# Gated linear attention on one core: chunks of 128 tokens with gates summed from the middle, one carried state instead of three

## The chip, the cores and the metric

The kernel runs on one core of one Trainium2 chip. The metric is device time in microseconds (us) of one execution. The kernel before took 1087.53 us, the median of three runs (1085.79 to 1088.14).

## The reference, cut to what matters

The program computes three transformer layers on 256 tokens of width 1024, in f32: a first block (convolution, sparse attention, feed-forward), a layer whose mixer is gated linear attention, and a layer with block attention. The change lies in the mixer of the second one. It has four heads, a key width of 128 and a value width of 256, and a gate per token and key channel:

```python
def gla_mixer(x, w_in, w_gk, b_gk, norm_g, w_out):
    q, k, v, g, gk_low = split_cols(x @ w_in, GLA_COLS)
    log_a = jax.nn.log_sigmoid((gk_low @ w_gk + b_gk).astype(jnp.float32)) / GLA_GATE_NORMALIZER
    q = to_heads(q, GLA_HEADS) * (GLA_DK ** -0.5)
    o = chunk_gla(q, to_heads(k, GLA_HEADS), to_heads(v, GLA_HEADS), to_heads(log_a, GLA_HEADS))
    o = from_heads(rms_norm_2(o.astype(x.dtype), norm_g)) * jax.nn.silu(g)
    return o @ w_out
```

`chunk_gla` evaluates the recurrence S_t = diag(exp(log_g_t)) S_{t-1} + k_t v_t^T, o_t = S_t^T q_t. The reference does so in chunks of 64 tokens: inside a chunk it forms causal scores from q * exp(cum) and k * exp(-cum), where cum is the running sum of the gates from the start of the chunk; between chunks it carries a state that is decayed by the chunk's whole gate and added to by the keys times exp(last - cum). The chunk length is a choice of the algorithm: any length gives the same outputs but for rounding.

## The kernel before, in words

All weights come from HBM as f32 in pieces of 128 x 2048 (`emit_raw`, line 111, three buffers) and each half of a piece, 128 x 1024, is split into a high and a low part: ScalarE writes the high part (`whi`, line 127), VectorE the rest (`wlo`, line 129). A projection is then three fp32r matmuls for every product (lines 168 to 170 where the weights are stationary, lines 174 to 176 where the activations are). The splits run up to five halves ahead of use. Work inside the attention itself uses plain f32 matmuls; each of them shows in the trace as two passes.

PSUM has four tiles for accumulation (`ps_acc`) and four work tiles (`ps_wk`), of 128 x 512 f32 each.

The 256 tokens are two token tiles of 128 (t = 0, 1). In the stage of the linear attention (lines 890 to 1048) the program goes through these steps:

- The q projection (line 938), the low-rank gate input (`pk`, line 943), and for each tile the gate logits (line 950) with their log-sigmoid: three ScalarE operations (lines 953 to 955) and one on VectorE (line 956) give `la`.
- For each tile, on TensorE: the running sum inside the two 64-token chunks of the tile (`pc`, line 960, with the constant matrix `tri`), the sum from a token to the end of its chunk (`pf`, line 961, with `suf`), and the total of each chunk for each head (`pdec`, line 964, four matmuls with two columns). ScalarE takes exponentials of them (line 967: `ecum`, `einv`, `esuf`; line 969: `dec`). ScalarE's order in this part is the program's own (`manual_schedule`); the others are ordered by the compiler's scheduler, by priority in program order.
- The v projection (two halves of 512 columns, line 981) and the k projection, whose evacuation multiplies by `einv` (line 977) and `esuf` (line 978, into `kend`).
- Transposes of the scaled q and k (line 988), copied to SBUF by ScalarE (line 990).
- The state after chunks 0, 1 and 2 (lines 993 to 1005): for each chunk and head one matmul of 64 rows, `kend` with v (line 998); for chunk 0 ScalarE copies the result (line 1002), for the others VectorE multiplies the state before by the decay and adds the new part (line 1004).
- Scores for each tile and head (line 1013), masked by a predicated copy on VectorE (line 1014) into a tile that was set to zero (line 1009). The mask keeps a pair of tokens only if both are in the same 64-token chunk.
- The outputs (lines 1018 to 1038, high priority): for each pair of heads and tile, scores times v (line 1027), plus for each 64-token chunk after the first the read of the state (line 1030), a matmul with 64 stationary columns that adds to 64 of the 128 output rows; then a sum of squares on ScalarE (line 1033), a power on GpSimd (line 226), and a scaling on VectorE (line 1037).
- The gate projection (`evac_g`, line 1043), two halves of 512 columns. Its matmuls depend on nothing of the attention, so the scheduler puts them between the attention's matmuls on TensorE. Its result is multiplied by the outputs and transposed for the output projection (line 1045, `to_T`, lines 238 to 244).

The output projection, a layer norm, the feed-forward part and the third layer follow. The output projection's early weight splits take over SBUF of the stage, among it the tags S0 and S1 of the state tiles.

Of the kernel before, what the change touches and what calls it, by code (L numbers as in the profile page):

```python
# [9 lines left out]
F32 = mybir.dt.float32  # L10
# [38 lines left out]
for _n, _w in (("ident", P), ("mask", 2 * P), ("tri", P), ("suf", P), ("ind", 2), ("m2", META),  # L49
               ("invf", 16), ("cq", L), ("sq", L), ("ci", L), ("si", L)):  # L50
    CST[_n] = _o
    _o += _w
# [25 lines left out]
def tile_hybrid(ctx: ExitStack, tc: tile.TileContext, x, meta, wts, misc, vec, cst, rows, gkw, ng, pos,  # L78
# [124 lines left out]
    tri = cs[:, CST["tri"]:CST["tri"] + P]  # L203
# [702 lines left out]
    V.tensor_scalar(mask_i, tri, 16.0, None, op0=OP.mult)  # L906
# [38 lines left out]
    dec = gp.tile([P, 4, 4], F32, name="dec")  # L945
    pdec = ps_wk()
    with tc.manual_schedule(engines={ENG.Activation}):
# [10 lines left out]
        for t in range(2):  # L958
            pc, pf = ps_wk(), ps_wk()
            PE.matmul(pc, tri, la[t], start=True, stop=True)  # L960
            PE.matmul(pf, suf, la[t], start=True, stop=True)
            for h in range(4):
                c = (h * 2 + t) * 2
                PE.matmul(pdec[:, c:c + 2], la[t][:, h * P:(h + 1) * P], ind, start=True, stop=True)
            for lst, src, s, nm in ((ecum, pc, 1.0, "ec"), (einv, pc, -1.0, "ei"), (esuf, pf, 1.0, "es")):
# [3 lines left out]
        A.activation(dec.rearrange("p a b -> p (a b)"), pdec[:, :16], AF.Exp)  # L969
        A.activation(cssn, cssn, AF.Sin)  # L970
        A.preload_act_table_set("silu_and_others")
    kend = [gp.tile([P, 512], F32, name=f"ke{t}", tag=f"la{t}") for t in range(2)]
# [3 lines left out]
    def evac_k(t, ps):  # L976
        V.tensor_mul(k_tok[t], ps, einv[t])
        V.tensor_mul(kend[t], ps, esuf[t])
# [13 lines left out]
    sts = {}  # L992
    for c in range(3):
        t, o = c // 2, 64 * (c % 2)
        s4 = gp.tile([P, 4, 256], F32, name=f"S{c}", tag=f"S{c}")
        for h in range(4):
            pu = ps_wk()
            PE.matmul(pu[:, :256], kend[t][o:o + 64, h * P:(h + 1) * P], v_tok[t][o:o + 64, h * 256:(h + 1) * 256],
                      start=True, stop=True)
            s = s4[:, h, :]  # L1000
            if c == 0:
                A.activation(s, pu[:, :256], AF.Copy)
            else:
                V.scalar_tensor_tensor(s, sts[c - 1, h], dec[:, h, c:c + 1], pu[:, :256], op0=OP.mult, op1=OP.add)
            sts[c, h] = s
# [13 lines left out]
    for g in range(2):  # L1019
        for t in range(2):  # L1020
            with tc.high_priority():
                po2 = ps_wk()
                st = sc.tile([P, 2, 2], F32, name="st4", tag="st4", bufs=2)
                for a in range(2):
                    h = 2 * g + a
                    po = po2[:, a * 256:(a + 1) * 256]
                    PE.matmul(po, sm[t * 4 + h], v_tok[t][:, h * 256:(h + 1) * 256], start=True, stop=True)
# [251 lines left out]
```

## Time and profile before

| | before |
|---|---|
| median of 3 runs | 1087.53 us (1085.79 to 1088.14) |
| profiled execution, its own time | 1089.07 us |
| span of the profiled execution | 1087.3 us |
| TensorE busy | 1069.2 us, 98% |
| VectorE busy | 741.3 us, 68% |
| ScalarE busy | 602.1 us, 55% |
| GpSimd busy | 39.3 us, 4% |
| instructions, matmul records | 17606, 7042 |

The span goes from the first to the last instruction of the program. The profile's page gives busy time for each engine (PE is TensorE, DVE is VectorE, ACT is ScalarE, POOL is GpSimd; PEld is the weight load of TensorE, which overlaps its matmuls) and the chain of work that ended last, followed back through whatever released each step. Views of the trace list the waits, the busy time in chosen stretches and the instructions in order of time. Matmuls are pipelined: the duration that is shown for one overlaps the next, so neither busy time nor duration is the time that a matmul occupies the array.

### The profile page before, as it was taken

What the parts mean: (1) busy time and instruction counts of PE and PEld (TensorE: products, weight loads), DVE (VectorE), ACT (ScalarE), POOL (GpSimd) and SP (SyncE); (2) the same over time, 40 slices, a digit from 0 to 9 for tenths busy, and PEclk for the clock granted to TensorE, in tenths of its full rate; (3) what the DMA queues carried; (4) which work ended last, traced back from release to release, by engine and by line L of the source; (5) the groups of instructions that cost most, each with busy time, mean ns of one, the idle gap of its engine ahead of it and who ended that gap; (6) DMA issues with size and microseconds to landing.
All of it is one profiled execution on the core that took longest, in us unless ns stands there. A gap on an engine that the chain in (4) does not pass through costs nothing.

```text
span 1087.3 us, 17606 instructions
## 1 busy us (share of the span) xinstructions
PE 1069.2 (98%) x7042; PEld 960.1 (88%) x7042; DVE 741.3 (68%) x1297; ACT 602.1 (55%) x1051; POOL 39.3 (4%) x45
## 2 busy tenths in 40 slices
PE   8999999999999999999999999999999999999997
PEld 7998998899899999977777899999888878999995
DVE  5899999994776767674566645547665666555555
ACT  6896698574555555566361544446256925444440
POOL 0121001100000000000000000000000000000000
PEclk8999999999999999999999999999999999999999
DMA  7885556464354555453434655557254436555541
GB/s 287 258 197 157 194 161 180 119 242 159 136 202 164 193 179 195 169 193 125 153 125 150 229 194 191 178 179 267 101 209 156 152 120 233 194 192 178 180 149 39
DMA packets 33333, 192.37 MB, mean 177 GB/s; under 512 B 3889, under 2 KB 7857, under 8 KB 12002
## 3 DMA queue, kind: packets, MB, share of 16 engines
q1 hardware_dynamic: 28002, 185.02, 49.0%
q0 software_dynamic: 5248, 6.23, 3.6%
q8 instruction: 55, 0.90, 0.3%
q14 instruction: 28, 0.23, 0.1%
HBM read 183.96 MB, written 1.05 MB: 170 GB/s over the span
## 4 chain that ended last, share of the span: by engine, by line
PE 88%; DVE 6%; ACT 2%; issue 2%; DMA 1%; POOL 0%; SPq 0%; DVEq 0%; ACTq 0%; POOLq 0%
PE ps_wk L170 11%; PE ps_wk L169 11%; PE ps_wk L168 11%; PE ps_acc L174 10%; PE ps_acc L175 10%; PE ps_acc L176 10%; PE ps_acc L168 4%; PE ps_acc L169 4%; PE ps_acc L170 4%; DVE wlo L129 1%; PE ps_wk L238 1%; DVE yc L350 1%; PE ps_acc L319 1%; ACT whi L127 1%; PE ps_wk L526 1%
## 5 line engine op out<-in xcount | busy, mean ns | idle before, releaser
L129 DVE TENSOR_TENSOR wlo<-wraw,whi 128x1024 fp32r<-128x1024 f32 x320 | 388.3, 1222 | 208.1 <-ACT whi L127 207.6
L127 ACT ACTIVATE whi<-wraw 128x1024 fp32r<-128x1024 f32 x322 | 337.5, 1059 | 304.2 <-PE ps_wk L169 116.2
L169 PE MATMUL ps_wk<-hT_l,whi 128*128 128x256 f32 (+1 forms) x976 | 274.8, 282 | 0.0
L170 PE MATMUL ps_wk<-hT_h,wlo 128*128 128x256 f32 (+1 forms) x976 | 274.6, 281 | 0.0
L168 PE MATMUL ps_wk<-hT_h,whi 128*128 128x256 f32 (+1 forms) x976 | 274.1, 281 | 0.0
L168 PEld LDWEIGHTS ps_wk<-hT_h,whi 128*128 128x128 f32 x976 | 184.4, 189 | 1.1
L169 PEld LDWEIGHTS ps_wk<-hT_l,whi 128*128 128x128 f32 x976 | 184.0, 189 | 1.4
L170 PEld LDWEIGHTS ps_wk<-hT_h,wlo 128*128 128x128 f32 x976 | 184.8, 189 | 0.3
L174 PE MATMUL ps_acc<-whi,rg_h 128*128 128x512 f32 x328 | 131.0, 400 | 0.0
L175 PE MATMUL ps_acc<-wlo,rg_h 128*128 128x512 f32 x328 | 129.6, 395 | 0.0
L176 PE MATMUL ps_acc<-whi,rg_l 128*128 128x512 f32 x328 | 127.1, 395 | 0.0
L168 PE MATMUL ps_acc<-hT_h,whi 128*128 128x258 f32 (+2 forms) x352 | 102.1, 290 | 0.0
L170 PE MATMUL ps_acc<-hT_h,wlo 128*128 128x258 f32 (+2 forms) x352 | 100.4, 285 | 0.0
L169 PE MATMUL ps_acc<-hT_l,whi 128*128 128x258 f32 (+2 forms) x352 | 100.4, 285 | 0.0
L176 PEld LDWEIGHTS ps_acc<-whi,rg_l 128*128 128x128 f32 x328 | 61.6, 188 | 14.8 <-DVE rg_l L195 0.2
L174 PEld LDWEIGHTS ps_acc<-whi,rg_h 128*128 128x128 f32 x328 | 61.6, 188 | 14.0 <-ACT rg_h L193 0.2
L175 PEld LDWEIGHTS ps_acc<-wlo,rg_h 128*128 128x128 f32 x328 | 61.7, 188 | 12.9
L174 PE MATMUL ps_acc<-whi,hT_h 128*128 128x512 f32 (+1 forms) x184 | 72.1, 392 | 0.0
L176 PE MATMUL ps_acc<-whi,hT_l 128*128 128x512 f32 (+1 forms) x184 | 71.6, 389 | 0.0
L175 PE MATMUL ps_acc<-wlo,hT_h 128*128 128x512 f32 (+1 forms) x184 | 71.3, 387 | 0.0
L169 PEld LDWEIGHTS ps_acc<-hT_l,whi 128*128 128x128 f32 x352 | 66.3, 188 | 0.3
L168 PEld LDWEIGHTS ps_acc<-hT_h,whi 128*128 128x128 f32 x352 | 66.2, 188 | 0.3
(939 smaller groups left out, 1570.5 us busy)
## 6 DMA issues: line engine op xcount, KB each, us to landing
wraw<-in_wts_dram SPq DMA_DIRECT2D x166, 1024.0 KB, 4.9
ysum<-zs POOLq DMA_DIRECT2D x10, 258.0 KB, 7.2
x<-in_x_dram SPq DMA_DIRECT2D x4, 512.0 KB, 3.6
lg<-in_rows_dram SPq DMA_DIRECT2D x4, 512.0 KB, 3.6
lb<-in_rows_dram SPq DMA_DIRECT2D x4, 512.0 KB, 4.6
wraw<-in_wts_dram SPq DMA_DIRECT2D x2, 512.0 KB, 7.0
out_dram<-x SPq DMA_DIRECT2D x4, 256.0 KB, 2.0
mraw<-in_misc_dram SPq DMA_DIRECT2D x1, 576.0 KB, 12.6
```

The source lines that it names most:

```text
L127: A.activation(hi, r, AF.Copy)
L129: V.tensor_sub(lo, r, hi.bitcast(F32))
L168: PE.matmul(ps, wh, xh, start=first, stop=False)
L169: PE.matmul(ps, wh, xl, start=False, stop=False)
L170: PE.matmul(ps, wl, xh, start=False, stop=last)
L174: PE.matmul(ps, xh, wh, start=first, stop=False)
L175: PE.matmul(ps, xh, wl, start=False, stop=False)
L176: PE.matmul(ps, xl, wh, start=False, stop=last)
L238: PE.transpose(pt[:, a, :], src[:, k * P:(k + 1) * P], ident)
L319: PE.matmul(ps[:, :L], w[a][:, k * P:(k + 1) * P], hT[b][:, k, :], start=k == 0 and a + b == 0, stop=k == KT - 1 and a == 1)
L350: tap = V.scalar_tensor_tensor(dst[:, b, :], src[:, b, :], wc[b], dst[:, b, :], op0=OP.mult, op1=OP.add)
L526: PE.matmul(po, vt[j][:, gs], pT[j + 1], start=False, stop=j == t)
```

## The change

The chunk is now a whole token tile of 128 tokens. The running sums of the gates are counted from the middle of the tile: the constant `rel` gives, for a token in the second half, the sum from token 64 up to it, and for one in the first half minus the sum from the token after it up to token 63. Both exponentials, exp(sum) for q and exp(-sum) for k, are then of sums over at most 64 tokens, as before. The mask becomes the plain causal one (made from `suf` in one operation). Only one state is carried, that at the end of tile 0, read by tile 1. So `pf`, `esuf` and `kend` are made for tile 0 alone; `pdec` for tile 1 alone, as the total of the first 64 tokens of tile 1, since the state must be brought to the middle of tile 1. The state is one matmul of 128 rows for each head (two heads in one PSUM tile), copied on ScalarE with the decay as a scale for each row. The state's read for tile 1 is one matmul of 128 columns for each head; tile 0 has none. SBUF tiles S1, S2, the second `esuf` and the second `kend` are gone.

```diff
--- before.py
+++ after.py
@@ -46,7 +46,7 @@
 
 CST = {}
 _o = 0
-for _n, _w in (("ident", P), ("mask", 2 * P), ("tri", P), ("suf", P), ("ind", 2), ("m2", META),
+for _n, _w in (("ident", P), ("mask", 2 * P), ("rel", P), ("suf", P), ("ind", 2), ("m2", META),
                ("invf", 16), ("cq", L), ("sq", L), ("ci", L), ("si", L)):
     CST[_n] = _o
     _o += _w
@@ -200,7 +200,7 @@
     cs = per.tile([P, CST["cq"]], F32, name="cs")
     ident = cs[:, CST["ident"]:CST["ident"] + P]
     vmask = cs[:, CST["mask"]:CST["mask"] + 2 * P]
-    tri = cs[:, CST["tri"]:CST["tri"] + P]
+    rel = cs[:, CST["rel"]:CST["rel"] + P]
     suf = cs[:, CST["suf"]:CST["suf"] + P]
     ind = cs[:, CST["ind"]:CST["ind"] + 2]
     m2 = cs[:8, CST["m2"]:CST["m2"] + META]
@@ -903,7 +903,7 @@
     nc.sync.dma_start(gw, gkw)
     ngb = row_bcast(gp, ng, 256, "ngb", 1)
     mask_i = gp.tile([P, P], I32, name="mask_i")
-    V.tensor_scalar(mask_i, tri, 16.0, None, op0=OP.mult)
+    V.tensor_scalar(mask_i, suf, -16.0, 1.0, op0=OP.mult, op1=OP.add)
     posi = bp.tile([P, 2], I32, name="posi")
     nc.sync.dma_start(posi, pos.rearrange("o (t p) -> p (o t)", p=P))
 
@@ -942,7 +942,7 @@
               k == 0, k == KT - 1)
     A.activation(gkT[0:16, :], pk[:16, :SEQ], AF.Copy)
     la, ecum, einv, esuf = [], [], [], []
-    dec = gp.tile([P, 4, 4], F32, name="dec")
+    dec = gp.tile([P, 4, 2], F32, name="dec")
     pdec = ps_wk()
     with tc.manual_schedule(engines={ENG.Activation}):
         for t in range(2):
@@ -956,26 +956,31 @@
             V.scalar_tensor_tensor(l_, pz, 0.0, z, op0=OP.min, op1=OP.subtract)
             la.append(l_)
         for t in range(2):
-            pc, pf = ps_wk(), ps_wk()
-            PE.matmul(pc, tri, la[t], start=True, stop=True)
-            PE.matmul(pf, suf, la[t], start=True, stop=True)
-            for h in range(4):
-                c = (h * 2 + t) * 2
-                PE.matmul(pdec[:, c:c + 2], la[t][:, h * P:(h + 1) * P], ind, start=True, stop=True)
-            for lst, src, s, nm in ((ecum, pc, 1.0, "ec"), (einv, pc, -1.0, "ei"), (esuf, pf, 1.0, "es")):
+            pc = ps_wk()
+            PE.matmul(pc, rel, la[t], start=True, stop=True)
+            out_ = [(ecum, pc, 1.0, "ec"), (einv, pc, -1.0, "ei")]
+            if t == 0:
+                pf = ps_wk()
+                PE.matmul(pf, suf, la[t], start=True, stop=True)
+                out_.append((esuf, pf, 1.0, "es"))
+            else:
+                for h in range(4):
+                    PE.matmul(pdec[:, 2 * h:2 * h + 2], la[t][:, h * P:(h + 1) * P], ind, start=True, stop=True)
+            for lst, src, s, nm in out_:
                 e = gp.tile([P, 512], F32, name=f"{nm}{t}", tag=f"{nm}{t}")
                 A.activation(e, src, AF.Exp, scale=s)
                 lst.append(e)
-        A.activation(dec.rearrange("p a b -> p (a b)"), pdec[:, :16], AF.Exp)
+        A.activation(dec.rearrange("p a b -> p (a b)"), pdec[:, :8], AF.Exp)
         A.activation(cssn, cssn, AF.Sin)
         A.preload_act_table_set("silu_and_others")
-    kend = [gp.tile([P, 512], F32, name=f"ke{t}", tag=f"la{t}") for t in range(2)]
+    kend = gp.tile([P, 512], F32, name="ke", tag="la0")
     for t in range(2):
         V.tensor_mul(q_tok[t], q_tok[t], ecum[t])
 
     def evac_k(t, ps):
         V.tensor_mul(k_tok[t], ps, einv[t])
-        V.tensor_mul(kend[t], ps, esuf[t])
+        if t == 0:
+            V.tensor_mul(kend, ps, esuf[0])
 
     for nn in range(2):
         xs_cols(hT, lambda t, ps, nn=nn: A.activation(v_tok[t][:, nn * 512:(nn + 1) * 512], ps, AF.Copy))
@@ -989,20 +994,14 @@
             o = gp.tile([P, 4, P], F32, name=f"{nm}T{t}", tag=f"{nm}{t}")
             A.activation(o.rearrange("p a b -> p (a b)"), pt, AF.Copy)
             lst.append(o)
-    sts = {}
-    for c in range(3):
-        t, o = c // 2, 64 * (c % 2)
-        s4 = gp.tile([P, 4, 256], F32, name=f"S{c}", tag=f"S{c}")
-        for h in range(4):
-            pu = ps_wk()
-            PE.matmul(pu[:, :256], kend[t][o:o + 64, h * P:(h + 1) * P], v_tok[t][o:o + 64, h * 256:(h + 1) * 256],
-                      start=True, stop=True)
-            s = s4[:, h, :]
-            if c == 0:
-                A.activation(s, pu[:, :256], AF.Copy)
-            else:
-                V.scalar_tensor_tensor(s, sts[c - 1, h], dec[:, h, c:c + 1], pu[:, :256], op0=OP.mult, op1=OP.add)
-            sts[c, h] = s
+    state4 = gp.tile([P, 4, 256], F32, name="S", tag="S0")
+    for h in range(0, 4, 2):
+        pu = ps_wk()
+        for a in range(2):
+            PE.matmul(pu[:, a * 256:(a + 1) * 256], kend[:, (h + a) * P:(h + a + 1) * P],
+                      v_tok[0][:, (h + a) * 256:(h + a + 1) * 256], start=True, stop=True)
+        for a in range(2):
+            A.activation(state4[:, h + a, :], pu[:, a * 256:(a + 1) * 256], AF.Copy, scale=dec[:, h + a, 0:1])
     sm = []
     for t in range(2):
         mt4 = gp.tile([P, 4, P], F32, name=f"sm{t}", tag=f"es{t}")
@@ -1024,11 +1023,9 @@
                 for a in range(2):
                     h = 2 * g + a
                     po = po2[:, a * 256:(a + 1) * 256]
-                    PE.matmul(po, sm[t * 4 + h], v_tok[t][:, h * 256:(h + 1) * 256], start=True, stop=True)
-                    for c in range(2):
-                        if 2 * t + c > 0:
-                            PE.matmul(po[64 * c:64 * c + 64], qd[t][:, h, 64 * c:64 * c + 64],
-                                      sts[2 * t + c - 1, h], start=False, stop=True, skip_group_check=True)
+                    PE.matmul(po, sm[t * 4 + h], v_tok[t][:, h * 256:(h + 1) * 256], start=True, stop=t == 0)
+                    if t == 1:
+                        PE.matmul(po, qd[t][:, h, :], state4[:, h, :], start=False, stop=True)
                     sq = bp.tile([P, 512], F32, name="sqw")
                     A.activation(sq[:, :256], po, AF.Square, accum_out=st[:, a, 0:1])
                 r = rsqrt(st[:, :, 1], st[:, :, 0], 1.0 / 256, EPS)
@@ -1240,10 +1237,10 @@
     i = np.arange(P)
     put("ident", np.eye(P, dtype=f))
     put("mask", np.concatenate([np.zeros((P, P)), np.where(i[None, :] <= i[:, None], 0.0, NEG)], axis=1))
-    same = (i[:, None] // 64) == (i[None, :] // 64)
-    put("tri", ((i[:, None] <= i[None, :]) & same) / 16.0)
-    put("suf", ((i[:, None] > i[None, :]) & same) / 16.0)
-    put("ind", (i[:, None] // 64 == np.arange(2)[None, :]) / 16.0)
+    a, b = i[:, None], i[None, :]
+    put("rel", (((a >= P // 2) & (a <= b)) * 1.0 - ((a < P // 2) & (a > b)) * 1.0) / 16.0)
+    put("suf", (a > b) / 16.0)
+    put("ind", np.repeat(a < P // 2, 2, axis=1) / 16.0)
     put("m2", np.where(np.arange(META)[None, :] <= META - 2 + np.arange(8)[:, None] % 2, 0.0, NEG))
     put("invf", np.tile((f(500000.0) ** (-np.arange(0, 32, 2, dtype=f) / f(32)))[None], (P, 1)))
     p = np.arange(L, dtype=f)
```

## Rows read from the trace of the kernel before

**Rows 1.** The page: busy time of each engine, and the chain that ended last by engine.
```profile
PE 1069.2 (98%) x7042; PEld 960.1 (88%) x7042; DVE 741.3 (68%) x1297; ACT 602.1 (55%) x1051; POOL 39.3 (4%) x45
...
PE 88%; DVE 6%; ACT 2%; issue 2%; DMA 1%; POOL 0%; SPq 0%; DVEq 0%; ACTq 0%; POOLq 0%
```

**Rows 2.** Windows of the stage: stretch, length, busy us (instructions), TensorE's granted clock, DMA share, GB/s.
```profile
486.00:550.00 64.00, 64.00 (x296) 47.01 (x295) 32.96 (x63) 32.77 (x59) 2.80 (x4) 1.00 0.37 132
535.80:541.00 5.20, 5.20 (x28) 3.12 (x26) 0.52 (x3) 0.47 (x2) 0.00 (x0) 1.00 0.00 0
541.00:549.00 8.00, 8.00 (x35) 4.63 (x35) 3.17 (x10) 3.33 (x14) 2.10 (x3) 1.00 0.00 0
```

**Rows 3.** Waits from 486 to 570 us: total, times, longest.
```profile
ACT whi L127 <- PE ps_acc L176: 11.2, 14, 5.4
...
ACT we0h L127 <- DMA wraw<-in_wts_dram: 1.6, 1, 1.6
```

**Rows 4.** TensorE's timeline, 490 to 497 us: start, length, engine, line, operation, tiles.
```profile
492.71 0.95 PE L964 MATMUL ps_wk<-cs,la 128*128 128x2 f32 x8
493.52 1.10 PE L960 MATMUL ps_wk<-la,cs 128*128 128x512 f32 x2
494.46 1.02 PE L961 MATMUL ps_wk<-la,cs 128*128 128x512 f32 x2
495.32 0.95 PE L964 MATMUL ps_wk<-cs,la 128*128 128x2 f32 x8
```

**Rows 5.** TensorE's timeline, 526 to 550 us.
```profile
529.16 4.60 PE L998 MATMUL ps_wk<-v,ke 64*128 64x256 f32 x24
533.69 0.94 PE L1013 MATMUL ps_wk<-ecT,eiT 128*128 128x128 f32 x6
534.38 0.48 PE L176 MATMUL ps_acc<-whi,hT_l 128*128 128x512 f32 x1
534.70 1.28 PE L1013 MATMUL ps_wk<-ecT,eiT 128*128 128x128 f32 x10
...
536.05 1.89 PE L1027 MATMUL ps_wk<-v,sm 128*128 128x256 f32 x8
537.87 1.94 PE L1030 MATMUL ps_wk<-S,ecT 128*64 128x256 f32 x12
539.74 0.70 PE L1027 MATMUL ps_wk<-v,sm 128*128 128x256 f32 x2
540.37 0.65 PE L1030 MATMUL ps_wk<-S,ecT 128*64 128x256 f32 x2
540.94 0.50 PE L175 MATMUL ps_acc<-wlo,hT_h 128*128 128x512 f32 x1
...
542.77 0.65 PE L1030 MATMUL ps_wk<-S,ecT 128*64 128x256 f32 x4
543.36 0.50 PE L174 MATMUL ps_acc<-whi,hT_h 128*128 128x512 f32 x1
```

**Rows 6.** Matmuls of L1027 and L1013: passes, duration ns min/median/max, first and last start.
```profile
L1027 PE MATMUL ps_wk<-v,sm x16: 378/379/483, 536.0 to 547.4; 128*128 128x256 f32 x16
...
L1013 PE MATMUL ps_wk<-ecT,eiT x16: 271/275/377, 533.7 to 535.7; 128*128 128x128 f32 x16
```

**Rows 7.** VectorE's timeline, 520 to 550 us.
```profile
531.24 3.22 DVE L1004 SCALAR_TENSOR_TENSOR S<-S,dec,ps_wk 128x256 f32<-128x256 f32 x8 [0.44 <-PE ps_wk L998]
534.38 1.94 DVE L1014 COPY_PREDICATED sm<-mask_i,ps_wk 128x128 f32<-128x128 int32 x8
```

**Rows 8.** ScalarE's timeline, 526 to 550 us.
```profile
527.00 1.06 ACT L127 ACTIVATE whi<-wraw 128x1024 fp32r<-128x1024 f32 x1 [0.33 <-PE ps_acc L176]
...
528.92 1.09 ACT L990 ACTIVATE eiT<-ps_wk 128x512 f32<-128x512 f32 x2
529.90 1.68 ACT L1002 ACTIVATE S<-ps_wk 128x256 f32<-128x256 f32 x4
```

**Rows 9.** ScalarE's scaled products of L367: count, duration ns min/median/max, shapes.
```profile
L367 ACT ACTIVATE zs<-hp,dwh x48: 482/495/520, 34.3 to 196.6; 128x258 f32<-128x258 f32 x20, 128x256 f32<-128x256 f32 x4, 128x248 f32<-128x248 f32 x4, 128x244 f32<-128x244 f32 x4
```

## The prediction

> **What bounds the kernel now.** I read the page first. TensorE is busy for 1069.2 us, 98% of the span, and the chain that ended last is 88% TensorE [rows 1]. A sum over the whole span says nothing about one stage, so the second view is the windows of the stage that the change edits. From 486 to 550 us TensorE is busy for all 64.0 us, VectorE for 33.0 and ScalarE for 32.8, the clock is granted in full, and the DMA share falls to 0.00 in both of its last stretches [rows 2]. So the weights stand ready there: the loads wait for buffers, not the buffers for loads. The waits say the same from the other side: ScalarE's weight splits wait 11.2 us in total for TensorE to give back a buffer, and only once, for 1.6 us, for a load [rows 3]. Here a microsecond that TensorE no longer needs should be a microsecond of the span, and work taken from VectorE or ScalarE should be worth nothing by itself.
>
> A busy share doesn't say how long a matmul holds the array, because its shown duration includes a tail that overlaps the next one. So I price by the TensorE timeline, from the start of one group to the start of the next [rows 4, 5]. An f32 matmul appears there as two passes; the counts below are passes. Three steps are needed. A full-array pass of 256 columns: the eight L1027 passes take 1.89 us, the last has the usual 0.38 [rows 6], so seven steps are 1.51, or **0.216 us** each. A 128-column score pass: ten take 1.28, the last 0.28 [rows 6], so (1.28 - 0.28) / 9 = 0.11. And the change of array shape: the first step after a change costs about 0.1 more. L1013's first six take 0.94, so five steps are 0.66 and not 0.56; from the last full L1027 pass (536.05 + 7 x 0.216 = 537.56) to the first L1030 pass it is 0.31 and not 0.216; the L1027 pair after L1030 takes 0.70, so its step is 0.32 [rows 5].
>
> **The change part by part, on TensorE.**
> 1. The suffix sum of the second token tile goes. L961 for tile 1 runs from 494.46 to 495.32 [rows 4]: **-0.86**.
> 2. The chunk totals of tile 0 go: L964's eight two-column passes from 492.71 to 493.52 [rows 4]: **-0.81**. Tile 1 keeps its eight. They stood between the cumulative sums of the two tiles, so L960 of tile 1 now comes at about 492.7 and needs the gates of tile 1; if those are late, projection passes stand behind it in the queue. I put nothing on this, and the bound is the 0.81 itself.
> 3. The state updates: 24 passes of 64 rows become 8 of 128 rows. Before, they run from 529.16 to 533.69, 4.53 us; after, 8 x 0.216 = 1.73, so -2.80. Both changes of shape around them go too, L988 to L998 and L998 to L1013, some 0.1 each: **-3.0** [rows 5].
> 4. The reads of the state: 24 passes with 64 output columns become 8 with 128, in the shape of L1027, and tile 0 needs none. The block of twelve takes 537.87 to 539.74 = 1.87 and becomes 4 x 0.216 = 0.86, with two changes of shape: -1.2. A pair for tile 0 (540.37 to 540.94, 0.57) goes with its two changes of shape: -0.77, and there are two of these. A four for tile 1 (542.77 to 543.36, 0.59) becomes 0.43: -0.16 and the two changes make -0.35, twice [rows 5]. Together 1.2 + 1.54 + 0.70 = **-3.4**.
>
> The sum is 0.86 + 0.81 + 3.0 + 3.4 = 8.1 us; 2 + 8 + 16 + 16 = 42 passes fewer.
>
> Here a rule can be set against the rows. L998's 24 half-height passes take 4.53 / 24 = 0.189 us each, hardly less than the 0.216 of a full pass: those of one chunk use the same half of the rows and follow each other, and only where one chunk's passes meet the next one's do they overlap. L1030 differs: four passes on the two column halves take 0.65, as two on one half do, so those do run side by side [rows 5]. The Trainium skill, "TensorEngine Tiling (Array Packing)", sections Overview and Key Properties, says that a contraction of 64 or less can gain up to 2x, as independent tiles load and multiply in parallel; that speaks against merging the halves. By that rule the 24 passes would cost 12 x 0.216 = 2.6, step 3 would give 0.9 without the changes of shape, and the whole about 6.0; the trace shows the gain on the columns (0.65 for four as for two), not on these rows.
>
> **Off the path.** VectorE loses the eight state updates of L1004, 3.22 us [rows 7], and one multiply into kend; ScalarE loses one exponential. They save nothing of themselves, since TensorE covers them. The four state copies of L1002 (1.68 us [rows 8]) stay on ScalarE but now scale by a column of dec. No row shows that form from PSUM: below it lies the plain copy (4 in 1.68, 0.43 a step), above it a scaled 258-column product of 0.495 [rows 9]. I take the plain copy, nearest in tile and source; the difference, 4 x 0.07 at most, lies on an idle engine. The mask and the table of constants cost what they did. No DMA is added, removed or moved past another.
>
> **What is late next.** The 4.53 us of state updates also covered ScalarE's copies of the transposed tiles, which end at 528.92 + 1.09 = 530.01 [rows 8], and the scores behind them need work tiles of PSUM, of which there are four. On the clock of before (all engines of the stage move up together), the shorter updates end at 529.16 + 1.73 = 530.89. Scores 1 and 2 find tiles free; scores 3 and 4 take those of the state copies, free at about 530.7 and 531.6, when they are due at 531.3 and 531.6. The masked copies then start 0.69 after the first score, as now (533.69 to 534.38), and follow at 1.94 / 8 = 0.24 [rows 5, 7]; the sixth ends near 531.58 + 6 x 0.24 = 533.0, when the eight scores end at about 532.8 and the four output heads of the first block want it. With some 0.2 for the hand-over I put **+0.4** on this. Bounds: 0, if a projection pass stands in the gap as L176 does now at 534.38 [rows 5], and 3.0, if the chain gives back all of step 3. Expected: 8.1 - 0.4 = **7.7 us** off the profiled execution's own time of 1089.07 (span 1087.3 and 1.8 around it), to 1081.4. The runs' median, 1087.53, is 1.5 below that execution; off the median the forecast is **1079.8 us**.
>
> **Rivals.**
> - **The cover is gone.** Copies, PSUM tiles and masked copies set the pace between the transposes and the first outputs, and step 3 returns most of its 3.0: 8.1 - 3.0 = 5.1, so about 1082.4. For it: the estimate has 0.0 to 0.4 us of slack in three places. Against: the gate projection, 96 matmuls, is at hand as filler, and the program puts some into such gaps today, at 534.38 and between the output heads [rows 5].
> - **Better than the sum.** The order of instructions is rebuilt for the whole program. If it then alternates less between the passes of the stage and those of the projection (a dozen such places between the transposes and the last output, some 0.1 us each as above) and no wait comes in step 3, the gain is 8.1 + 1.2: 1078.2. Little speaks for it, as the output heads still wait for one another and the projection still fills between them.
> - **Weights set the pace.** TensorE comes to the later projections 8 us earlier and finds them not loaded: 1087.5, no change. It needs loads that run without pause; against it stands the share of 0.00 for 13.2 us [rows 2] and one wait of 1.6 us for a load [rows 3].
> - **Slower: ScalarE's queue.** The second tile's outputs now depend on ScalarE alone for the state. If each of the two pairs of copies is placed behind a weight split that waits for a buffer (longest such wait 5.4 us [rows 3], split 1.06 [rows 8]) and TensorE has nothing else queued, it stalls 2 x 6.5 = 13 us: 1087.5 - 8.1 + 13 = 1092. It decides once such stalls pass 8.1 us. Against it: the copies run today in one row right behind the transposes, with no split among them [rows 8].
>
> **How the numbers follow.** A measurement of this kernel can tell about 0.2%, 2.2 us, from no change. Chances: the forecast 0.62, the cover 0.20, better 0.08, weights 0.06, slower 0.04. The forecast's own range is 1078.5 to 1081.5; the first rival with its 3.0 bound and some scatter of runs (1085.8 to 1088.1 before) reaches 1083.2, and the better case, with the same scatter, makes the low end 1077.3. That leaves the last two cases and the tails outside. Faster by over 0.2%: 0.62 + 0.20 + 0.08 = 0.90; same 0.06; slower 0.04.
>
> **What would show it.** Right: TensorE has 42 matmul records fewer (up to missing ones); one L961 pair; eight passes at the new state line in about 1.7 us; no 64-row or 64-column group left in the stage; TensorE's busy time falls by some 8 us with no new idle time over 0.5 us; the stretch after the stage is as long as before. Wrong: a wait of TensorE for the masked copies or the state copies of over 1 us, scores that stand apart by more than 0.3, a DMA wait ahead of the splits after the stage, or a later stage that is longer than before and gives the gain back.

## The result, and the profile after

The changed kernel takes 1081.43 us, the median of six runs (1079.86 to 1081.98), against 1087.84 for six runs of the kernel before beside it (1085.79 to 1091.3). The ratio is 0.993 with a 95% interval of 0.9916 to 0.9944, a gain of 6.1 to 9.1 us: faster, as the whole interval lies below 1. The profiled execution took 1080.53 us (span 1078.7), 8.5 less than the one of before.

The first line of the page of after answers to [rows 1]: 42 matmul records fewer, and 9.2 us of TensorE's busy time.

```profile
PE 1060.0 (98%) x7000; PEld 956.7 (89%) x7000; DVE 737.9 (68%) x1288; ACT 601.9 (56%) x1050; POOL 39.3 (4%) x45
```

TensorE's timeline of after answers to [rows 4, 5]: start, length, engine, line, operation, tiles. First the gate sums:

```profile
490.20 1.10 PE L960 MATMUL ps_wk<-la,cs 128*128 128x512 f32 x2
491.13 1.02 PE L964 MATMUL ps_wk<-la,cs 128*128 128x512 f32 x2
491.99 1.02 PE L960 MATMUL ps_wk<-la,cs 128*128 128x512 f32 x2
492.85 0.95 PE L968 MATMUL ps_wk<-cs,la 128*128 128x2 f32 x8
```

One suffix sum (L964 here) and one group of totals (L968) are left, and the second running sum follows without a gap, 0.86 behind the suffix sum. Then the state, the scores and the outputs:

```profile
526.60 1.89 PE L1001 MATMUL ps_wk<-v,ke 128*128 128x256 f32 x8
528.33 0.83 PE L1012 MATMUL ps_wk<-ecT,eiT 128*128 128x128 f32 x6
528.92 0.48 PE L176 MATMUL ps_acc<-whi,hT_l 128*128 128x512 f32 x1
529.23 1.35 PE L1012 MATMUL ps_wk<-ecT,eiT 128*128 128x128 f32 x10
530.42 1.89 PE L1026 MATMUL ps_wk<-v,sm 128*128 128x256 f32 x8
532.15 1.03 PE L1028 MATMUL ps_wk<-S,ecT 128*128 128x256 f32 x4
...
534.37 0.40 PE L175 MATMUL ps_acc<-wlo,hT_h 128*128 128x512 f32 x1
534.68 0.70 PE L1026 MATMUL ps_wk<-v,sm 128*128 128x256 f32 x2
...
536.57 0.40 PE L174 MATMUL ps_acc<-whi,hT_h 128*128 128x512 f32 x1
536.99 0.70 PE L1026 MATMUL ps_wk<-v,sm 128*128 128x256 f32 x2
...
538.47 0.40 PE L176 MATMUL ps_acc<-whi,hT_l 128*128 128x512 f32 x1
538.92 0.70 PE L1026 MATMUL ps_wk<-v,sm 128*128 128x256 f32 x2
...
542.66 0.40 PE L174 MATMUL ps_acc<-whi,hT_h 128*128 128x512 f32 x1
543.23 0.66 PE L238 MATMUL ps_wk<-cs,gs 128*128 128x128 f32 x4 [0.17 <-DVE gs L1042]
```

The state group lasts from 526.60 to 528.33, 1.73 us where it was 4.53, and no 64-row or 64-column shape is left. The reads of the state (L1028) keep the shape of what stands before them. The waits of after, 486 to 562 us (total, times, longest), answer to [rows 3]:

```profile
ACT whi L127 <- PE ps_acc L176: 11.0, 14, 5.4
...
DVE sm L1013 <- PE ps_wk L1012: 1.7, 2, 1.6
ACT we0h L127 <- DMA wraw<-in_wts_dram: 1.6, 1, 1.6
...
PEld ps_wk L1026 <- ACT sqw L1030: 1.3, 3, 0.5
```

The weight splits wait as before. The wait for a load is still 1.6 us (a second one, of 0.3, is new). At the scores VectorE waits for TensorE, not the other way round. The last row is new in size. In the waits of before, same stretch, the same wait was about half:

```profile
PEld ps_wk L1027 <- ACT sqw L1033: 0.7, 3, 0.3
```

There an output head starts 0.24 behind the projection pass ahead of it, as TensorE's timeline of before has it; in the rows of after above it is 0.31, 0.42 and 0.45.

```profile
541.98 0.40 PE L176 MATMUL ps_acc<-whi,hT_l 128*128 128x512 f32 x1
542.22 0.63 PE L1027 MATMUL ps_wk<-v,sm 128*128 128x256 f32 x2
```

To place the gain I cut the stage at four points: the first gate-logit pass (L950), the first transpose, the first score, the first output matmul, and as its end the first add of the layer norm behind the output projection. All of the kernels that follow stand in one table; what lies behind the stage takes 504.3 to 504.5 us in each, and TensorE's granted clock is 1.00 in the stage of every one.

| profiled execution | start of stage | to transposes | to scores | to outputs | to norm add | stage | own time |
|---|---|---|---|---|---|---|---|
| before | 486.81 | 39.99 | 6.89 | 2.36 | 46.86 | 96.09 | 1089.07 |
| after | 486.09 | 38.23 | 4.01 | 2.09 | 43.98 | 88.31 | 1080.53 |
| e1_gate_sums | 485.97 | 40.00 | 4.00 | 2.09 | 43.90 | 89.99 | 1082.06 |
| e2_half_rows | 485.12 | 38.24 | 4.42 | 3.00 | 43.88 | 89.54 | 1080.78 |
| e3_half_rows_turns | 486.62 | 38.23 | 4.43 | 2.90 | 43.87 | 89.43 | 1082.22 |
| e4_half_cols | 486.70 | 38.25 | 4.00 | 2.09 | 45.74 | 90.08 | 1082.86 |
| e5_vector_updates | 484.49 | 38.23 | 4.01 | 4.59 | 41.77 | 88.60 | 1079.24 |
| e6_no_suffix | 488.84 | 37.42 | 4.00 | 2.09 | 43.92 | 87.43 | 1082.39 |
| e7_both_heads | 487.11 | 38.25 | 4.00 | 2.09 | 43.74 | 88.08 | 1081.31 |
| e8_both | 486.33 | 37.43 | 4.00 | 2.09 | 43.67 | 87.19 | 1079.80 |
| e9_before_pairs | 487.30 | 39.99 | 6.23 | 3.05 | 46.88 | 96.15 | 1089.61 |
| e10_state_twice | 484.30 | 38.25 | 5.74 | 1.78 | 43.89 | 89.66 | 1080.05 |
| e11_vector_from_psum | 486.15 | 38.25 | 4.01 | 4.33 | 41.85 | 88.44 | 1080.82 |

From before to after the stage loses 7.78 us: 1.76 ahead of the transposes, 2.88 to the scores, 0.27 to the outputs, 2.88 behind. The other 0.7 of the 8.5 lies ahead of the stage, where both kernels run the same code. The start of the stage differs by up to 4.5 us between these executions (484.30 to 488.84), so the experiments are read by the stage and not by the own time. Each is one execution, but parts that an edit leaves alone repeat closely: ahead of the transposes, eight of the kernels agree within 0.02 us (38.23 to 38.25).

### The profile page after: what moved, and what is told of

It reads as the page before. It is cut to its first block, busy times and chain, and to the rows that moved or that the text cites. A ratio compares the mean times of both kernels' runs of the same rounds, so it can differ in the third digit from the quotient of the medians.

```text
span 1078.7 us, 17504 instructions
## 1 busy us (share of the span) xinstructions
PE 1060.0 (98%) x7000; PEld 956.7 (89%) x7000; DVE 737.9 (68%) x1288; ACT 601.9 (56%) x1050; POOL 39.3 (4%) x45
## 3 DMA queue, kind: packets, MB, share of 16 engines
q0 software_dynamic: 5248, 6.23, 3.6%
## 5 line engine op out<-in xcount | busy, mean ns | idle before, releaser
L176 PE MATMUL ps_acc<-whi,rg_l 128*128 128x512 f32 x328 | 127.1, 395 | 0.0
L176 PEld LDWEIGHTS ps_acc<-whi,rg_l 128*128 128x128 f32 x328 | 61.6, 188 | 14.8 <-DVE rg_l L195 0.2
L176 PE MATMUL ps_acc<-whi,hT_l 128*128 128x512 f32 (+1 forms) x184 | 71.4, 388 | 0.0
```

The lines of the kernel that those rows point to most:

```text
L176: PE.matmul(ps, xl, wh, start=False, stop=last)
```

## The experiments

The theory is that of the prediction: the stage is bound by TensorE, and what the change gives is the time of the passes that it saves. Against it stand that VectorE's chain, the updates and then the masked copies, was what the state group gave back; that half-height passes need not have cost what they did, so that the merge of the halves gave nothing; and that TensorE fills any gap with projection passes, so that passes more or less are worth little. Edits are against the changed kernel unless said otherwise.

**The gate sums put back.** Steps 1 and 2 undone: suffix sum and totals for both tiles.

```diff
...
-            if t == 0:
-                pf = ps_wk()
...
-            else:
-                for h in range(4):
-                    PE.matmul(pdec[:, 2 * h:2 * h + 2], la[t][:, h * P:(h + 1) * P], ind, start=True, stop=True)
+            pf = ps_wk()
+            PE.matmul(pf, suf, la[t], start=True, stop=True)
+            out_.append((esuf, pf, 1.0, "es"))
+            for h in range(4):
+                c = 8 * t + 2 * h
+                PE.matmul(pdec[:, c:c + 2], la[t][:, h * P:(h + 1) * P], ind, start=True, stop=True)
...
```

> The stage is measured from the first pass of the gate logits (L950) to the first add of the layer norm behind it (L763): 96.10 us in the kernel before (486.81 to 582.91), 88.32 after (486.09 to 574.41). Here the suffix sum of tile 1 and the chunk totals of tile 0 are computed again, and thrown away. Theory (TensorE's passes set the stage, each part is worth its passes): 88.32 + 0.86 + 0.81 = 90.0. Rival (the gate sums lie beside ScalarE's exponentials, and the gain came from the state alone): 88.3 to 88.9, the one exponential of 0.6 at most.

The stage is 1.68 us longer. TensorE's timeline of this kernel shows the two groups that came back:

```profile
491.87 0.95 PE L968 MATMUL ps_wk<-cs,la 128*128 128x2 f32 x8
...
493.62 1.02 PE L964 MATMUL ps_wk<-la,cs 128*128 128x512 f32 x2
```

Steps 1 and 2 hold: all of it lies ahead of the transposes (40.00 against 38.23), and nothing covers it.

**The state's passes twice.** Each pair of state matmuls is repeated into a work tile that nothing reads.

```diff
+        pv = ps_wk()
+        for a in range(2):
+            PE.matmul(pv[:, a * 256:(a + 1) * 256], kend[:, (h + a) * P:(h + a + 1) * P],
+                      v_tok[0][:, (h + a) * 256:(h + a + 1) * 256], start=True, stop=True)
```

> The kernel after, in which each state matmul is done a second time into a work tile that nothing reads: eight more passes of 128 rows, and nothing more for VectorE or ScalarE. Theory (a pass on this stage is worth its 0.216 us): 8 x 0.216 = +1.73, stage 90.0. Rival (what the state part gave came from VectorE's updates and the work tiles that they held, and the passes lay beside that): 88.3 to 88.6.

```profile
524.83 1.03 PE L1001 MATMUL ps_wk<-v,ke 128*128 128x256 f32 x4
525.69 1.03 PE L1005 MATMUL ps_wk<-v,ke 128*128 128x256 f32 x4
...
528.28 1.95 PE L1016 MATMUL ps_wk<-ecT,eiT 128*128 128x128 f32 x16
```

In TensorE's timeline the group takes 528.28 - 524.83 = 3.45, twice 1.73. The first score comes 1.73 later (5.74 against 4.01), but the stage grows by 1.35 only. The sixteen score passes now run in one piece, 0.31 shorter, and the projection pass that after has between them (L176) moves behind the outputs. It costs nothing there: it fills the gap in which after has TensorE wait for the gated outputs (L238, 0.57 behind the pass before it in the rows of after, 0.32 here). A pass saved is worth its time where it stands, less what gaps further on give back, and the rival of passes without value falls.

**VectorE's work put back, without its passes.** Eight products on VectorE between the state copies and the masked copies, as long as the updates that were removed. Their result is not read.

```diff
...
+    for c in range(2):
+        for h in range(4):
+            V.scalar_tensor_tensor(spare[:, h, :], state4[:, h, :], ones_c, state4[:, h, :],
+                                   op0=OP.mult, op1=OP.add)
```

> The kernel after, and VectorE does eight products of 128 x 256 into a spare tile between the state copies and the masked copies, where the eight state updates stood before (0.42 us each, 3.3 in all). Theory (TensorE's passes set the stage): VectorE's work is worth nothing as long as it is covered, but the 4.53 us of passes that covered it are gone; the masked copies start some 2.5 to 3 us later, and of that the projection passes cover what the order lets them: stage 88.3 to 89.5. Rival (the gain of the state part came from VectorE's chain being gone): stage 91.2, nearly all of the 2.9 us that the state part gave.

VectorE's timeline:

```profile
526.57 3.25 DVE L1010 SCALAR_TENSOR_TENSOR spare<-S,ones_c 128x256 f32<-128x256 f32 x8 [0.99 <-ACT S L1007]
529.75 1.17 DVE L1020 COPY_PREDICATED sm<-mask_i,ps_wk 128x128 f32<-128x128 int32 x5
```

The eight take 3.25 us, as [rows 7] has 3.22, and the masked copies follow directly behind. The stage grows by 0.29 alone: the outputs start 2.50 later and the rest behind them is 2.21 shorter, since 11 projection passes stand between the first score and the first output where after has one.

The next kernel holds PSUM's work tiles as well, as the old updates did: the state is made by eight VectorE steps from PSUM, and ScalarE has no part in it.

```diff
...
-            A.activation(state4[:, h + a, :], pu[:, a * 256:(a + 1) * 256], AF.Copy, scale=dec[:, h + a, 0:1])
+            for o in (spare, state4):
+                V.scalar_tensor_tensor(o[:, h + a, :], pu[:, a * 256:(a + 1) * 256], dec[:, h + a, 0:1], zero,
+                                       op0=OP.mult, op1=OP.add)
```

> The kernel after, in which VectorE makes the state from the two work tiles in eight steps of 128 x 256 (each product done twice, the first into a spare tile), and ScalarE makes no copies: TensorE has no pass more than after, but the work tiles are held by a VectorE chain of 3.3 us, as in the kernel before. With the same chain on SBUF the stage was 88.60, 0.29 over after. Theory (as long as projection passes are at hand, the order fills such a hold): 88.6 to 88.9. Rival (holding the work tiles was a limit of its own in the kernel before): +1.2 to +2.5, stage 89.5 to 90.8, with waits of the scores on VectorE.

VectorE's timeline, the first of the eight steps and the first masked copies:

```profile
527.75 0.48 DVE L1008 SCALAR_TENSOR_TENSOR spare<-ps_wk,dec,zero 128x256 f32<-128x256 f32 x1 [0.48 <-PE ps_wk L1004]
...
530.89 0.69 DVE L1018 COPY_PREDICATED sm<-mask_i,ps_wk 128x128 f32<-128x128 int32 x3
```

The stage grows by 0.13, again with 11 projection passes between the first score and the first output. In the changed kernel VectorE's chain is covered by the projection even where it holds the tiles, so its absence is not what the gain came from.

**The state by half-height passes.** Here the rule of the Trainium skill that the prediction weighed against the rows is tested by itself: one state, but each head's contraction in two halves of 64 rows, into two work tiles. The first form runs the two heads on one half of the rows, then on the other; the second takes the halves in turns.

```diff
-        pu = ps_wk()
+        pu = [ps_wk(), ps_wk()]
+        for a, c in ((0, 0), (1, 0), (0, 1), (1, 1)):   # second form: (0, 0), (0, 1), (1, 0), (1, 1)
+            part = slice(64 * c, 64 * c + 64)
+            PE.matmul(pu[c][:, a * 256:(a + 1) * 256], kend[part, (h + a) * P:(h + a + 1) * P],
+                      v_tok[0][part, (h + a) * 256:(h + a + 1) * 256], start=True, stop=True)
...
-            A.activation(state4[:, h + a, :], pu[:, a * 256:(a + 1) * 256], AF.Copy, scale=dec[:, h + a, 0:1])
+            s = state4[:, h + a, :]
+            A.activation(s, pu[0][:, a * 256:(a + 1) * 256], AF.Copy, scale=dec[:, h + a, 0:1])
+            V.scalar_tensor_tensor(s, pu[1][:, a * 256:(a + 1) * 256], dec[:, h + a, 0:1], s, op0=OP.mult, op1=OP.add)
```

> The eight state passes of 128 rows become 16 of 64 rows, per pair of heads first both upper halves, then both lower halves, in two PSUM tiles that VectorE adds. Theory A (half-height passes follow each other and overlap only where the next one in the queue uses the other half): 16 x 0.216 less some 0.3 at each of three meetings, so 2.5 to 2.6 us for the group, +1 us on the stage: 89.3. Theory B (row halves never share the array): 3.5 us, stage 90.2. Theory C (independent tiles run side by side, whatever the order): 1.8 us, stage 88.5.

> The same 16 passes, upper and lower half in turns. Theory A (neighbours on different halves overlap): about 1.8 to 2.0 us for the group, stage 88.5. Theory B (never): 3.5 us, stage 90.2. Theory C: as the kernel of the other order, 1.8 us. So A sets this one apart from the one before, B and C make both alike.

TensorE's timeline of the first form:

```profile
525.73 2.10 PE L1002 MATMUL ps_wk<-v,ke 64*128 64x256 f32 x16
527.78 1.35 PE L1015 MATMUL ps_wk<-ecT,eiT 128*128 128x128 f32 x6
```

and of the second:

```profile
527.23 2.01 PE L1002 MATMUL ps_wk<-v,ke 64*128 64x256 f32 x16
529.29 1.03 PE L1015 MATMUL ps_wk<-ecT,eiT 128*128 128x128 f32 x4
```

Sixteen half-height passes take 2.05 and 2.06 us, 0.13 each, and not 16 x 0.189 = 3.0 as in [rows 5]. Two halves do run side by side, in either order (TensorE's queue has the matmuls in the order written); the group costs 0.32 more than eight full passes, of which the two changes of shape are some 0.2. The rule of the Trainium skill, "TensorEngine Tiling (Array Packing)", Key Properties, that different tiles work in parallel, agrees with these rows; what the prediction made of [rows 5] does not hold for half rows in general. Of the 1.1 to 1.2 us that the stage grew by, 0.8 to 0.9 lie between the first score and the first output, where two engines now have to empty the work tiles and the scores wait for them. From the waits of the first form, 520 to 535 us:

```profile
DVE S L1007 <- ACT S L1006: 1.2, 1, 1.2
...
PEld ps_wk L1015 <- ACT S L1006: 0.4, 1, 0.4
```

**Why then were the halves of before apart?** Before has three chunks of four heads, and each head took a whole work tile, of which there are four. Chunk 0 fills them all, so chunk 1 cannot start next to it on the other half of the rows: its first pass stands at 530.33 in the trace of before, 1.17 behind that of chunk 0, when the first of ScalarE's state copies (from 529.90, 0.43 a step [rows 8]) is done. Against the kernel before, two heads now share a tile:

```diff
-            pu = ps_wk()
-            PE.matmul(pu[:, :256], kend[t][o:o + 64, h * P:(h + 1) * P], v_tok[t][o:o + 64, h * 256:(h + 1) * 256],
-                      start=True, stop=True)
+            if h % 2 == 0:
+                pu2 = ps_wk()
+                for b in range(2):
+                    PE.matmul(pu2[:, b * 256:(b + 1) * 256], kend[t][o:o + 64, (h + b) * P:(h + b + 1) * P],
+                              v_tok[t][o:o + 64, (h + b) * 256:(h + b + 1) * 256], start=True, stop=True)
+            pu = pu2[:, (h % 2) * 256:(h % 2 + 1) * 256]
...
```

> The kernel before, in which two heads of a chunk's state update share one PSUM work tile, as in the change. The halved state passes of the kernel after ran side by side in either order, so what made the kernel before take 4.53 us for 24 half-height passes should be the work tiles: a chunk's four heads took all four. Theory: with two tiles a chunk, the upper-half passes of chunk 0 and the lower-half ones of chunk 1 run side by side, and the group takes 16 x 0.216 and some 0.2 = 3.6 us, chunk 2 being on the upper rows again: stage 95.2 instead of 96.1. Rival (passes on rows of one chunk and the next overlap no more than before): 4.5 us, stage 96.1.

TensorE's timeline, and then the wait at its scores from 526 to 550 us:

```profile
529.65 3.94 PE L1000 MATMUL ps_wk<-v,ke 64*128 64x256 f32 x24
533.52 0.71 PE L1016 MATMUL ps_wk<-ecT,eiT 128*128 128x128 f32 x4
534.43 0.49 PE L1016 MATMUL ps_wk<-ecT,eiT 128*128 128x128 f32 x2 [0.20 <-DVE S L1007]
```

```profile
PEld ps_wk L1016 <- DVE S L1007: 0.7, 2, 0.4
```

The group falls from 4.53 to 3.87 us, so the tiles did keep halves apart. That is near the least it can be: chunks 0 and 2 both lie on the upper rows, and 16 passes there, one behind the other, make 16 x 0.216 = 3.46 without the changes of shape. But the stage is as long as before (96.15). From the first score to the first output it takes 3.05 where it was 2.36: the scores now wait for VectorE's updates, TensorE is idle for 0.20, and three projection passes stand there in place of two. So in before the passes and VectorE's chain were about equally late. Better packing of the halves alone gives nothing in that kernel, in the order that it was compiled to, while two states fewer relieve both engines.

**The reads of the state by half columns.** Step 4 undone, with one state: each read as two matmuls of 64 stationary columns.

```diff
...
-                        PE.matmul(po, qd[t][:, h, :], state4[:, h, :], start=False, stop=True)
+                        for c in range(2):
+                            PE.matmul(po[64 * c:64 * c + 64], qd[t][:, h, 64 * c:64 * c + 64],
+                                      state4[:, h, :], start=False, stop=True, skip_group_check=True)
```

> The state is read by tile 1 in two matmuls of 64 stationary columns for each head, as before the change, instead of one of 128. Theory (column halves run side by side, and only the changes of array shape cost): four separate groups with two changes each, 8 x 0.1 = +0.8 on the stage, 89.1; a group of four passes takes as long as two did, 0.43. Rival (halves in sequence): 8 more passes x 0.216 = 1.7 and the changes, 90.8.

TensorE's timeline:

```profile
532.86 1.08 PE L1029 MATMUL ps_wk<-S,ecT 128*64 128x256 f32 x4
533.87 0.70 PE L1026 MATMUL ps_wk<-v,sm 128*128 128x256 f32 x2
...
537.29 0.65 PE L1029 MATMUL ps_wk<-S,ecT 128*64 128x256 f32 x4
537.88 0.50 PE L176 MATMUL ps_acc<-whi,hT_l 128*128 128x512 f32 x1
```

The stage is 1.77 us longer where 0.8 was expected. A group of four passes takes 1.01 us in the first row and 0.59 in the third. The compiled order of TensorE's queue explains it. The first group holds one half of two heads and the second group the other half of the same two, with full-width passes (L1026) between them; passes on one half follow one another. In the later two groups both halves of one head stand together and run side by side. So the merge is worth its changes of shape at least, and where the order keeps the halves apart, the saved passes too.

**What could still go.** If the gates of tile 0 are counted from its middle, the keys scaled for the scores can serve for the state too, with the decay from the middle of one tile to the middle of the next. The suffix sum, its exponential and `kend` then go.

```diff
-            if t == 0:
-                pf = ps_wk()
-                PE.matmul(pf, suf, la[t], start=True, stop=True)
...
+            half = slice(64, 128) if t == 0 else slice(0, 64)
+            V.tensor_copy(mid[half], l_[half])
...
-            PE.matmul(pu[:, a * 256:(a + 1) * 256], kend[:, (h + a) * P:(h + a + 1) * P],
+            PE.matmul(pu[:, a * 256:(a + 1) * 256], k_tok[0][:, (h + a) * P:(h + a + 1) * P],
...
```

> One more step in the direction of the change: no suffix sum at all. The state is made from the keys times exp(-sum) that are there anyway, and the decay that its copy applies is the total of the second half of tile 0 and the first half of tile 1, from a tile into which VectorE copies these two halves of the gates. Theory (passes set the stage): two passes of 512 columns fewer, 0.86 us: stage 87.5. Rival (the sums of tile 1 wait for its gates: TensorE took them right when they were ready): the time goes into a gap ahead of them, stage 88.0 to 88.3.

The stage is 0.88 us shorter, the price of one suffix sum as in step 1.

In the next one both heads' output matmuls stand ahead of the two sums of squares, so that the second head's passes need not wait for ScalarE:

```diff
                         PE.matmul(po, qd[t][:, h, :], state4[:, h, :], start=False, stop=True)
+                for a in range(2):
+                    po = po2[:, a * 256:(a + 1) * 256]
                     sq = bp.tile([P, 512], F32, name="sqw")
```

> The kernel after, with the sums of squares of a pair of heads written behind the matmuls of both heads. Where the hand-over that the prediction put at 0.4 us shows in the trace of after is not at the scores but at three places in the output block, where a head's matmul waits for ScalarE's sum of squares (1.3 us in total, of which 0.08 to 0.22 a place reach the passes). Theory (that wait is real and comes from the head before in the same PSUM tile): the waits and the alternation with projection passes there go, 0.5 + 3 x 0.2: stage 87.2 to 87.6. Rival (it is only moved, since the outputs still need work tiles): 88.3.

In TensorE's timeline the output block is one run, with no projection pass inside:

```profile
531.45 2.32 PE L1026 MATMUL ps_wk<-v,sm 128*128 128x256 f32 x10
...
536.45 0.58 PE L174 MATMUL ps_acc<-whi,hT_h 128*128 128x512 f32 x1
```

The wait of L1026 for the squares is gone from the list of waits, but the stage gains only 0.23. The waits of 520 to 545 us name what came in its place, the transposes of the gated outputs:

```profile
PEld ps_wk L238 <- DVE gs L1044: 1.2, 1, 1.2
```

Both edits together:

> The version without the suffix sum (stage 87.43) and with both heads' matmuls ahead of their sums of squares (88.08) in one kernel; after is 88.32. Theory (the two lie in different parts of the stage and add up): 88.32 - 0.88 - 0.24 = 87.2, and 8.9 us less than before: ratio to the kernel before 0.992. Rival (they don't add up): 87.4. Either is within the scatter of the runs to the kernel after; the stage in the trace tells them apart.

The stage is 87.19 us, 1.12 less than after. Over six runs, though, the median is 1081.55 us (1079.8 to 1083.95), a ratio of 0.994 (0.9926 to 0.9955) to before: the whole program's time can't be told from that of the changed kernel. The stage is better; a gain on the program is not shown.

## Why the prediction was right

The forecast was faster, 1079.8 us, and 1081.43 lies in its range. By the medians the gain is 6.4 us, 1.3 less than the 7.7 of the forecast, which the scatter ahead of the stage can make; the median alone would not decide between it and the first rival, the cover gone (1082.4). The stage does: it lost 7.78 us where the forecast had 7.7 and that rival 5.1, and no wait at the scores took anything back. That 7.78 meets 7.7 so closely is in part luck, since the 0.4 that the forecast took off for one wait was lost in another place.

- **The bound.** TensorE's passes set the stage. Passes added without other work (the state twice) cost 1.35 of their 1.73, the rest going into a gap behind the outputs; VectorE work added without passes costs 0.29 of its 3.25. ScalarE's scaled copies, in its timeline of after, take what the plain ones took [rows 8], so the nearest row was the right choice:

```profile
527.67 1.70 ACT L1004 ACTIVATE S<-ps_wk,dec 128x256 f32<-128x256 f32 x4
```

- **Steps 1 and 2**, -1.67: measured -1.76 in the stage, 1.68 when put back.
- **Step 3**, -3.0: measured -2.88 up to the first score and -0.27 from there to the first output. Of the 0.27, 0.10 is the second change of shape (the first six scores take 528.92 - 528.33 = 0.59, in before 0.69 [rows 5]), so the step gave 2.98; the rest comes of one projection pass that no longer stands between the scores but behind the outputs. The size is right, the reading of the rows half right. The half-height passes of before cost 0.189 each because each chunk took all four work tiles, not because halves of the rows can't overlap. The prediction's 2.6 for 24 overlapped passes paired them all, but two chunks of the three lie on the same rows, so at least 3.46 was left; sharing the tiles brought them to 3.87. Most of the gain is two states of three going away, 16 passes of 24: one state by half rows takes 2.05, by full rows 1.73.
- **The hand-over**, +0.4: the place was wrong, and the size fits only because another wait, that of step 4, cost about as much; this is the luck in the number. Between scores and outputs nothing was lost; the copies of the state and the masked copies came in time.
- **Step 4**, -3.4: measured -2.88 behind the first output. The passes and changes of shape are priced right: summed over the four groups of heads, without the projection passes between them, TensorE needs 3.3 us less. The prediction counted no added wait between these groups. With fewer passes in them, ScalarE's sums of squares come later than TensorE wants the next head: L1026 waits 1.3 us for them in place of 0.7. In the rows of after, three heads start 0.31, 0.42 and 0.45 behind the projection pass before them; in before it was 0.23 or 0.24 each time. That is 0.47 in all, nearly the whole of the missing half microsecond. The kernel with both heads ahead of their squares has no such gaps, but its stage got back only 0.23, as a wait for the transposes took their place.
- **The rivals.** The chain of VectorE (the cover) fell by two kernels. Weights: the wait for a load stayed at 1.6 us beside a new one of 0.3, and what follows the stage is as long as before. ScalarE's queue: splits wait 11.0 us, as before, and TensorE waits for none of them. Better than the sum: the stage lost 7.78 us and not the 9.3 of that case; the waits of the outputs became longer, not shorter.

## What to carry to other kernels

Price an edit on a TensorE-bound stage by the steps from one group's start to the next, in that stage's own rows, and price the engines beside it at nothing only as long as independent passes can be queued into the gaps; adding the suspected work alone, with its result unread, is the cheapest way to see which it is. A row that shows passes following each other does not say that they must: look at what they write to before you take it for a property of the array. And compare stages, not totals, when a part of the program that was not touched varies by as much as the edit gives or more.

## What the runs showed of the hardware

**The scatter sits in the granted clock, ahead of the stage.** The stage started between 484.30 and 488.84 us in 13 executions with the same code ahead of it, while what lies behind it stayed within 0.2. Windows of three kernels (stretch, length, busy time and count of PE, PEld, DVE, ACT, POOL, granted clock, DMA share, GB/s) show where. After:

```profile
10.00:25.00 15.00, 14.07 (x84) 12.24 (x83) 10.06 (x16) 10.46 (x17) 0.00 (x0) 0.77 0.76 296
166.00:172.00 6.00, 6.00 (x37) 4.69 (x37) 5.70 (x16) 4.42 (x12) 0.06 (x1) 1.00 0.53 181
```

The kernel without the suffix sum, which started the stage last:

```profile
10.00:25.00 15.00, 14.71 (x77) 12.62 (x77) 10.05 (x17) 10.11 (x17) 0.00 (x0) 0.66 0.75 293
166.00:172.00 6.00, 6.00 (x16) 2.94 (x16) 3.89 (x9) 2.51 (x6) 0.00 (x0) 0.72 0.83 234
```

The kernel with the state twice, which started it first:

```profile
10.00:25.00 15.00, 14.05 (x104) 12.69 (x103) 12.29 (x19) 11.24 (x19) 0.00 (x0) 1.00 0.94 366
```

A mean between 0.5 and 1.0 says that the clock was at 1.2 GHz for a part of the stretch and at 2.4 for the rest: in windows of 2 us, after has 0.50 from 12 to 16 us and 1.00 from 18 us on. From 10 to 16 us, where their clocks already differ, the three have the same DMA share, 0.96 to 1.08. With 0.66 TensorE got 77 matmuls done in the first stretch, with 0.77 84, with 1.00 104. Kernels that differ only 300 us later got different clocks there, so an execution's total carries up to 4.5 us that no edit made. What decides the clock was not tried.

**Half tiles overlap by what stands next to them.** Row halves ran side by side once there were work tiles for both, in turns or two matmuls of one half before two of the other (0.13 us a pass); column halves did when both stood in one group (four passes in 0.59 us), and not when full-width passes lay between them (1.01).
